# HGRN2 on one NeuronCore: a level's products and elementwise steps for both halves of the tokens at once

## The chip, the cores and the metric

The kernel is one program on one NeuronCore of a Trainium2 chip. A core has five engines that run their own instruction streams and wait for each other through semaphores: TensorE (PE in the rows; its weight loads are listed as PEld), VectorE (DVE), ScalarE (ACT), GpSimd (POOL) and SyncE (SP, which issues most transfers). The metric is the device time of one execution in microseconds (us); lower is better.

## The reference, cut to what matters

Four layers of a decoder trunk run over 1024 tokens of width 1024, each with a normalisation before it and a gated residual add behind it. Layers 0 and 3 use HGRN2, layer 1 windowed attention, layer 2 gated DeltaNet. The change touches HGRN2 alone (8 heads of 128 channels, chunks of tokens):

```python
def hgrn2_scan(q, k, v, log_f):
    ...
    def step(S, inp):
        q_, k_, v_, lf = inp
        b = jnp.cumsum(lf, axis=-2)
        diff = b[..., :, None, :] - b[..., None, :, :]
        dec = jnp.exp(jnp.where(causal[:, :, None], diff, -jnp.inf))
        A = jnp.einsum('bhtd,bhsd,bhtsd->bhts', q_, k_, dec)
        o = jnp.einsum('bhts,bhse->bhte', A, v_) + jnp.einsum('bhtd,bhde->bhte', q_ * jnp.exp(b), S)
        b_last = b[..., -1:, :]
        S = jnp.exp(b_last)[..., 0, :, None] * S + jnp.einsum('bhsd,bhse->bhde', k_ * jnp.exp(b_last - b), v_)
        return S, o
```

The matrix A weighs token t against an earlier token s with a product of decays that differs from channel to channel, so it is no plain matmul.

## The kernel before, in words

The 1024 tokens are two halves of 512 (`HT`), a half is four chunks of 128 (`NC`). Arrays lie with channels on the 128 partitions and tokens along the free axis.

`hgrn2` works head by head. For each head two generators are woven together by `weave`, which takes the next piece from the stream that is least far along: `mix(h)`, the recurrence of head h, and `proj` and `proj_v`, the input projections of the next head (and of the z gate), with a few pieces of the next layer's modulation (`side`) between them. The projections are long rows of fp32r matmuls (`proj_ps` of 512 columns, `projt_ps` of 256), three for each product because weights and activations are split into a high and a low part (L196 to L198). What is written here only sets priorities: Tile, the layer that schedules the program, orders each engine's instructions when the program is built. Level products stand in `burst()`, a priority raised by 4000, so that they go as soon as they are ready; `mix` as a whole is raised by 150 (`PRH`).

`mix` does this for one half at a time (`for hf in halves`), in this order:

- **levels.** A is built inside each 128-token chunk by products over blocks of 2, 8, 32 and 128 tokens. Level 0 multiplies q against kg (16 small matmuls of 48 columns into `lev_ps`, L1004); VectorE takes the diagonal (L1010) and the neighbour (L1012, a predicated copy under `lmask`) into `hg_A`. Then, for l = 1, 3, 5: ScalarE and VectorE form `hg_X` from `hg_qf` and the decays `hg_F` (L1031 to L1033), TensorE multiplies X against kg (16 matmuls, L1004; for l = 5 twelve of 96, 64 or 32 columns, L1050), VectorE takes three pieces into A (L1039), and VectorE brings F, qf and kg up by two levels (L1056 to L1061). The products of a level read kg as the level before left it, and kg may be changed only when they are done.
- **at.** At l = 5 GpSimd copies A into the diagonal blocks of `hg_at` (four copies, L1044) and ScalarE copies the products into the others (three copies, L1053).
- **scan.** Transposes of kg (L1067), then chunk by chunk the output (`o_ps`: S times qf, L1077, and v times at, L1078) and the state (`s_ps`, L1082, and `hg_S`, L1087), then the norm, a transpose back (L1099) and the gate (L1102).

So a head runs levels of half 0, scan of half 0, levels of half 1, scan of half 1. `hg_q`, `hg_f`, `hg_kg` and `hg_qf` are tiles of one half, in three buffers each. The last head (h = 7) calls `mix` for each half by itself, beside the output projection.

Of the kernel before, what the change touches and what calls it, by code (L numbers as in the profile page):

```python
# [84 lines left out]
class Trunk:  # L85
# [175 lines left out]
    def level_masks(self):  # L261


        nc, const = self.nc, self.const
        si, ti, a, b = (self.np.tile([P, P], I32, name=f"lm{n}") for n in range(4))
        nc.gpsimd.iota(si, pattern=[[0, P]], base=0, channel_multiplier=1)
        nc.gpsimd.iota(ti, pattern=[[0, NC], [1, 32]], base=0, channel_multiplier=0)
        nc.vector.tensor_scalar(si, si, 31, None, ALU.bitwise_and)
        lmask = const.tile([P, 7 * 64], U8, name="lmask")
        self.eye32 = const.tile([P, P], F32, name="eye32")  # L270
        nc.vector.tensor_tensor(a, ti, si, ALU.subtract)
        nc.vector.tensor_scalar(self.eye32, a, 0, None, ALU.is_equal)
# [651 lines left out]
    def hgrn2(self, i, side):  # L924
# [4 lines left out]
        mp = st.enter_context(self.tc.tile_pool(name=f"hg{i}", bufs=1, reuse_waits="tile"))  # L929
        nc = self.nc  # L930
        H, HA, NG = 8, 7, 4 * NC
        bufs = {"X": 1, "q": 3, "f": 3, "kg": 3, "qf": 3, "tmp": 3, "v": 3, "zs": 3, "kht": 1, "ohi": 1, "olo": 1}

        def tl(tag, dt=F32):
            return mp.tile([P, HT], dt, name=f"hg_{tag}", tag=tag, bufs=bufs[tag])

        def proj(h, d, parts, halves=(0, 1)):

            def ev_q(hf, ps):
                sg = tl("tmp")  # L940
                nc.scalar.activation(sg, ps, AF.Sigmoid)
                d["q", hf] = mp.tile([P, NG, 48], F32, name="hg_q", tag="q", bufs=bufs["q"])
                gr = lambda x: x.rearrange("p (g t) -> p g t", g=NG)
                nc.vector.tensor_tensor(d["q", hf][:, :, :32], gr(ps), gr(sg), ALU.mult)

            def ev_f(hf, ps):
                f, kg, qf = tl("f"), tl("kg"), tl("qf")
# [7 lines left out]
                q = d["q", hf]  # L955
# [5 lines left out]
                d["f", hf], d["kg", hf], d["qf", hf] = f, kg, qf  # L961
# [28 lines left out]
        def mix(h, d, halves=(0, 1)):  # L990
            S = d.get("S")
            for hf in halves:
                q, f, kg, qf, v = (d[x, hf] for x in ("q", "f", "kg", "qf", "v"))
                at = ats[hf]
                A = mp.tile([P, P], F32, name="hg_A", tag="hg_A", bufs=2)

                def products(x, kg):

                    pl = self.psum("lev", "lev_ps", 2)[:, :192]
                    with self.burst():  # L1000
                        for c in range(NC):
                            for g in range(4):
                                gs = slice(g * 32, (g + 1) * 32)
                                nc.tensor.matmul(pl[gs, c * 48:(c + 1) * 48], kg[:, c * P + g * 32:c * P + (g + 1) * 32], x[:, 4 * c + g, :], start=True, stop=True)  # L1004
                    return pl


                pl = products(q, kg)
                pv = pl.rearrange("p (c t) -> p c t", c=NC)
                nc.vector.tensor_tensor(A.rearrange("p (c t) -> p c t", c=NC), pv[:, :, :32], self.eye32.rearrange("p (c t) -> p c t", c=NC), ALU.mult)  # L1010
                av = A.rearrange("p (c n b) -> p c n b", c=NC, b=2)[:, :, :, 1]
                nc.vector.copy_predicated(av, self.lmask[0, 1].rearrange("p (c n) b j -> p c (n b j)", c=NC), pv[:, :, 32:])  # L1012
                yield 700
                fv, kv = (x.rearrange("p (n b) -> p n b", b=2) for x in (f, kg))
                F = mp.tile([P, HT // 2], F32, name="hg_F", tag="hg_F", bufs=2)
                nc.vector.tensor_tensor(F, fv[:, :, 0], fv[:, :, 1], ALU.mult)
                nc.vector.tensor_tensor(kv[:, :, 0], kv[:, :, 0], fv[:, :, 1], ALU.mult)
# [3 lines left out]
                for l in (1, 3, 5):  # L1021
                    j = 1 << l
                    nq = HT // (4 * j)
                    qv, kv = (x.rearrange("p (n b j) -> p n b j", b=4, j=j) for x in (qf, kg))
                    Fv = F.rearrange("p (n b) -> p n b", b=4)
                    bc = lambda b0, b1, w: Fv[:, :, b0:b1, None].to_broadcast([P, nq, w, j])

                    nx = 7 if j == 32 else 6
                    X = mp.tile([P, NC * 7 * 32], F32, name="hg_X", tag="hg_X", bufs=bufs["X"])[:, :nq * nx * j]
                    xv = X.rearrange("p (n b j) -> p n b j", b=nx, j=j)  # L1030
                    nc.scalar.copy(xv[:, :, 0:3, :], qv[:, :, 1:4, :])  # L1031
                    nc.vector.tensor_tensor(xv[:, :, 3:5, :], qv[:, :, 2:4, :], bc(1, 3, 2), ALU.mult)
                    nc.vector.tensor_tensor(xv[:, :, nx - 1, :], xv[:, :, 4, :], bc(1, 2, 1)[:, :, 0, :], ALU.mult)  # L1033
                    if j < 32:
                        pl = products(X.rearrange("p (g t) -> p g t", g=NG), kg)
                        pv = pl.rearrange("p (n b j) -> p n b j", b=6, j=j)
                        av = A.rearrange("p (n b j) -> p n b j", b=4, j=j)
                        for n, b0 in ((1, 0), (2, 3), (3, 5)):
                            nc.vector.copy_predicated(av[:, :, n:, :], self.lmask[l, n], pv[:, :, b0:b0 + 4 - n, :])  # L1039
                        yield 700  # L1040
                    else:
                        for g in range(4):
                            gs = slice(g * 32, (g + 1) * 32)
                            nc.gpsimd.tensor_copy(at[gs, :, gs], A[gs].rearrange("p (c t) -> p c t", c=NC))  # L1044
                        pl = self.psum("lev", "lev_ps", 2).rearrange("p (c b t) -> p c b t", c=NC, t=32)
                        with self.burst():
                          for c in range(NC):
                            for g in range(3):
                                gs = slice(g * 32, (g + 1) * 32)
                                nc.tensor.matmul(pl[gs, c, g + 1:, :], kg[:, c * P + g * 32:c * P + (g + 1) * 32], xv[:, c, g::3 if g == 0 else 4 - g, :][:, :3 - g, :] if g < 2 else xv[:, c, 2:3, :], start=True, stop=True)  # L1050
                        for g in range(3):
                            gs = slice(g * 32, (g + 1) * 32)
                            nc.scalar.copy(at[gs, :, (g + 1) * 32:], pl[gs, :, g + 1:, :].rearrange("p c b t -> p c (b t)"))  # L1053
                        yield 900
                    for b in (2, 1):
                        nc.vector.tensor_tensor(Fv[:, :, b], Fv[:, :, b], Fv[:, :, b + 1], ALU.mult)  # L1056
                    nc.vector.tensor_tensor(qv[:, :, 1, :], qv[:, :, 1, :], bc(0, 1, 1)[:, :, 0, :], ALU.mult)
                    nc.vector.tensor_tensor(qv[:, :, 2:4, :], xv[:, :, 3::nx - 4, :], bc(0, 1, 2), ALU.mult)
                    nc.vector.tensor_tensor(kv[:, :, 0:3, :], kv[:, :, 0:3, :], bc(1, 4, 3), ALU.mult)
                    Fn = mp.tile([P, nq], F32, name="hg_F", tag=f"hg_F{l}", bufs=2)  # L1060
                    nc.vector.tensor_tensor(Fn, Fv[:, :, 0], Fv[:, :, 1], ALU.mult)  # L1061
                    F = Fn
                    yield 1
# [60 lines left out]
        drain(side)  # L1124
        for hf in range(2):
# [322 lines left out]
```

## Time and profile before

| | |
|---|---|
| median of 3 runs | 2753.58 us (2751.43 to 2759.05) |
| profiled execution: its time, its span | 2752.67 us, 2751.0 us |
| PE busy | 2669.9 us, 97% |
| PEld busy | 2147.2 us, 78% |
| DVE busy | 2001.3 us, 73% |
| ACT busy | 1224.1 us, 44% |
| POOL busy | 133.8 us, 5% |
| mean granted TensorE clock | 0.993 |

The span runs from the first to the last instruction, so the execution's time is a little longer. Busy times are unions of instruction spans; a matmul's span is longer than its spacing to the next, since matmuls overlap, so a busy PE need not be at its peak. Layer 0's heads run from about 64 to 530 us of the span, layer 3's from about 2185 to 2640 us, and each layer's last head and output projection follow.

### The profile page before, as it was taken

The numbers are of one execution on the slowest core, as the hardware profiler recorded it, in microseconds if no ns is written. First come the engines' busy times: TensorE is split into PE (matmuls) and PEld (weight loads), VectorE is DVE, ScalarE is ACT, GpSimd is POOL, SyncE is SP. The second block draws the span as 40 slices with busy tenths as digits, with TensorE's granted clock in tenths as the row PEclk, the third lists the DMA queues.
The fourth block names the chain that finished last, engine by engine and source line by source line (L and its number), as shares of the span: only waits on it lengthen the run. The fifth ranks groups of instructions, "written<-read, shape, count | busy, mean of one in ns | idle before, by whom it ended". The sixth has DMA issues, their size and how long they took to land.

```text
span 2751.0 us, 51716 instructions
## 1 busy us (share of the span) xinstructions
PE 2669.9 (97%) x19217; PEld 2147.2 (78%) x19217; DVE 2001.3 (73%) x5669; ACT 1224.1 (44%) x3107; POOL 133.8 (5%) x352
## 2 busy tenths in 40 slices
PE   8999999998999999899999999999999999999999
PEld 4878888778878767677788877787778888887877
DVE  6685765778677778677898798988875757556575
ACT  4332333444445565444546455555543433333342
POOL 0000100000000000001101001100000000000000
PEclk9999999999999999999999999999999999999999
DMA  6232222344223243324343343432463211111133
GB/s 237 82 103 82 66 85 74 118 129 146 62 85 97 77 149 91 116 74 111 94 127 101 92 123 101 116 104 77 150 188 119 81 54 40 51 46 49 46 120 112
DMA packets 347666, 273.30 MB, mean 99 GB/s; under 512 B 68963, under 2 KB 276246, under 8 KB 347414
## 3 DMA queue, kind: packets, MB, share of 16 engines
q1 hardware_dynamic: 347126, 268.95, 32.8%
q8 instruction: 151, 2.47, 0.4%
q14 instruction: 101, 0.83, 0.1%
q0 software_dynamic: 288, 1.05, 0.1%
HBM read 224.77 MB, written 45.15 MB: 98 GB/s over the span
## 4 chain that ended last, share of the span: by engine, by line
PE 76%; DVE 11%; DMA 6%; ACT 4%; issue 2%; SPq 1%; POOL 0%; DVEq 0%; ACTq 0%
PE proj_ps L196 10%; PE proj_ps L198 10%; PE proj_ps L197 10%; PE outp_ps L198 4%; PE outp_ps L196 4%; PE outp_ps L197 4%; PE projt_ps L197 3%; PE projt_ps L198 3%; PE projt_ps L196 3%; DMA ada_w<-in_ada_w_dram 2%; PE lev_ps L1004 2%; DVE gd_tb L617 1%; PE pv_ps L1330 1%; DVE w_lo L172 1%; PE w_ps L859 1%
## 5 line engine op out<-in xcount | busy, mean ns | idle before, releaser
L196 PE MATMUL proj_ps<-hhi,w_hi 128*128 128x512 f32 x1664 | 686.1, 412 | 11.2 <-ACT gd_tb L615 8.6
L197 PE MATMUL proj_ps<-hlo,w_hi 128*128 128x512 f32 x1664 | 675.5, 406 | 0.0
L198 PE MATMUL proj_ps<-hhi,w_lo 128*128 128x512 f32 x1664 | 674.0, 405 | 0.0
L196 PEld LDWEIGHTS proj_ps<-hhi,w_hi 128*128 128x128 f32 x1664 | 315.5, 190 | 68.3 <-ACT gd_tb L615 11.0
L198 PEld LDWEIGHTS proj_ps<-hhi,w_lo 128*128 128x128 f32 x1664 | 314.9, 189 | 59.1 <-issue 1.2
L197 PEld LDWEIGHTS proj_ps<-hlo,w_hi 128*128 128x128 f32 x1664 | 315.3, 190 | 53.0 <-issue 1.4
L172 DVE TENSOR_TENSOR w_lo<-w_raw,w_hi 128x512 fp32r<-128x512 f32 x332 | 223.1, 675 | 168.2 <-ACT w_hi L171 165.6
L171 ACT CAST w_hi<-w_raw 128x512 fp32r<-128x512 f32 x332 | 201.9, 611 | 307.8 <-PE proj_ps L197 183.1
L197 PE MATMUL projt_ps<-w_lo,hhi 128*128 128x256 f32 x896 | 256.1, 290 | 5.8 <-DVE w_lo L172 5.8
L196 PE MATMUL projt_ps<-w_hi,hhi 128*128 128x256 f32 x896 | 256.1, 291 | 0.5 <-ACT w_hi L171 0.5
L198 PE MATMUL projt_ps<-w_hi,hlo 128*128 128x256 f32 x896 | 255.4, 290 | 0.0
L196 PE MATMUL outp_ps<-o_hi,w_hi 128*128 128x512 f32 x576 | 229.3, 400 | 2.9 <-ACT o_hi L1156 1.9
L198 PE MATMUL outp_ps<-o_hi,w_lo 128*128 128x512 f32 x576 | 228.0, 398 | 1.4 <-DVE w_lo L175 1.4
L197 PE MATMUL outp_ps<-o_lo,w_hi 128*128 128x512 f32 x576 | 228.8, 398 | 0.2
L197 PEld LDWEIGHTS projt_ps<-w_lo,hhi 128*128 128x128 f32 x896 | 170.7, 192 | 9.2 <-DVE w_lo L172 6.8
L196 PEld LDWEIGHTS projt_ps<-w_hi,hhi 128*128 128x128 f32 x896 | 170.5, 192 | 3.8 <-issue 1.2
L198 PEld LDWEIGHTS projt_ps<-w_hi,hlo 128*128 128x128 f32 x896 | 170.6, 192 | 2.3 <-issue 1.4
L617 DVE SCALAR_TENSOR_TENSOR gd_tb<-gd_xs,taps,gd_tb 128x512 f32<-128x512 f32 x192 | 144.2, 751 | 25.1 <-ACT gd_tb L615 21.5
L174 ACT ACTIVATE w_hi<-w_raw,par 128x512 fp32r<-128x512 f32 (+1 forms) x136 | 94.7, 698 | 142.9 <-PE outp_ps L197 98.8
L196 PEld LDWEIGHTS outp_ps<-o_hi,w_hi 128*128 128x128 f32 x576 | 108.6, 189 | 27.0 <-ACT o_hi L1156 3.9
L175 DVE SCALAR_TENSOR_TENSOR w_lo<-w_raw,par,w_hi 128x512 fp32r<-128x512 f32 (+1 forms) x136 | 96.8, 716 | 42.8 <-ACT w_hi L174 41.5
L198 PEld LDWEIGHTS outp_ps<-o_hi,w_lo 128*128 128x128 f32 x576 | 108.6, 189 | 24.2 <-DVE w_lo L175 1.9
(388 smaller groups left out, 4918.5 us busy)
## 6 DMA issues: line engine op xcount, KB each, us to landing
ada_w<-in_ada_w_dram SPq DMA_DIRECT2D x160, 256.0 KB, 2.8
w_raw<-in_hg_in_w_dram SPq DMA_DIRECT2D x136, 256.0 KB, 2.8
w_raw<-in_gd_in_w_dram SPq DMA_DIRECT2D x108, 256.0 KB, 3.1
o_in<-od SPq DMA_DIRECT2D x72, 256.0 KB, 3.3
w_raw<-in_gd_out_w_dram SPq DMA_DIRECT2D x64, 256.0 KB, 2.8
w_raw<-in_sw_in_w_dram SPq DMA_DIRECT2D x48, 256.0 KB, 3.0
w_raw<-in_hg_out_w_dram SPq DMA_DIRECT2D x40, 256.0 KB, 2.9
ada_w<-in_ada_w_dram SPq DMA_DIRECT2D x8, 1024.0 KB, 10.0
```

The source lines that it names most:

```text
L171: nc.scalar.copy(hi, raw)
L172: nc.vector.tensor_tensor(lo, raw, hi.bitcast(F32), ALU.subtract)
L174: nc.scalar.activation(hi, raw, AF.Copy, scale=scale)
L175: nc.vector.scalar_tensor_tensor(lo, raw, scale, hi.bitcast(F32), ALU.mult, ALU.subtract)
L196: mm(out, a[0], b[0], start=start, stop=False)
L197: mm(out, a[0], b[1], start=False, stop=False)
L198: mm(out, a[1], b[0], start=False, stop=stop)
L617: nc.vector.scalar_tensor_tensor(y, xs[:, j:j + HT], w(j), y, ALU.mult, ALU.add)
L859: nc.tensor.matmul(po[:, hd[a]], dd["u"][a, hf][:, cs], rhs, start=True, stop=True)
L1004: nc.tensor.matmul(pl[gs, c * 48:(c + 1) * 48], kg[:, c * P + g * 32:c * P + (g + 1) * 32], x[:, 4 * c + g, :], start=True, stop=True)
L1330: nc.tensor.matmul(po[a * 64:(a + 1) * 64], vg[:, n + 1 - nkb + b, :], p4[:, :, a, :], start=b == 0, stop=b == nkb - 1)
```

## The change

A new generator `levels(d, halves)` does the levels and the at copies for all given halves before any scan; `mix` calls it first and keeps only the scan in its loop over halves. For heads 0 to 6 both halves are given, so A, X and F are twice as wide, 32 products of 48 columns go into one `lev_ps` tile, and each elementwise instruction covers 1024 tokens in place of 512. At l = 5 there is one `lev_ps` tile for each half, and the GpSimd and ScalarE copies stay apart by half. q, f, kg and qf become tiles of 1024 tokens, one buffer for even and one for odd heads (the even heads' in a pool of their own, `mp0`, closed after head 6). The masks get the double width, the unit mask `eye32` is 32 columns read again and again. The last head still gives one half at a time.

```diff
-        bufs = {"X": 1, "q": 3, "f": 3, "kg": 3, "qf": 3, "tmp": 3, "v": 3, "zs": 3, "kht": 1, "ohi": 1, "olo": 1}
+        bufs = {"X": 1, "tmp": 3, "v": 3, "zs": 3, "kht": 1, "ohi": 1, "olo": 1}
...
-                f, kg, qf = tl("f"), tl("kg"), tl("qf")
+                if hf == 0:
+                    d.update((x, (mp if h % 2 else mp0).tile([P, T], F32, name="hg_" + x, tag=x, bufs=1)) for x in ("f", "kg", "qf"))
+                f, kg, qf = (d[x][:, hf * HT:(hf + 1) * HT] for x in ("f", "kg", "qf"))
...
+        def levels(d, halves):
+
+            C, c0 = NC * len(halves), NC * halves[0]
+            W = C * P
...
+            def products(x):
+
+                pl = self.psum("lev", "lev_ps", 2)[:, :C * 48]
+                with self.burst():
+                    for c in range(C):
+                        for g in range(4):
+                            gs = slice(g * 32, (g + 1) * 32)
+                            nc.tensor.matmul(pl[gs, c * 48:(c + 1) * 48], kg[:, c * P + g * 32:c * P + (g + 1) * 32], x[:, 4 * c + g, :], start=True, stop=True)
+                return pl
...
+            yield 700 * len(halves)
...
+            for l in (1, 3, 5):
+                j = 1 << l
+                nq = W // (4 * j)
...
+                nc.scalar.copy(xv[:, :, 0:3, :], qv[:, :, 1:4, :])
+                nc.vector.tensor_tensor(xv[:, :, 3:5, :], qv[:, :, 2:4, :], bc(1, 3, 2), ALU.mult)
...
+                else:
+                    pls = [self.psum("lev", "lev_ps", 2).rearrange("p (c b t) -> p c b t", c=NC, t=32) for hf in halves]
+                    with self.burst():
+                        for c in range(C):
+                            for g in range(3):
+                                gs = slice(g * 32, (g + 1) * 32)
+                                x = (xv[:, c, 0:7:3, :], xv[:, c, 1:5:3, :], xv[:, c, 2:3, :])[g]
+                                nc.tensor.matmul(pls[c // NC][gs, c % NC, g + 1:, :], kg[:, c * P + g * 32:c * P + (g + 1) * 32], x, start=True, stop=True)
+                    for hf, pl in zip(halves, pls):
...
+                        for g in range(4):
+                            gs = slice(g * 32, (g + 1) * 32)
+                            nc.gpsimd.tensor_copy(ats[hf][gs, :, gs], Ah[gs])
+                        for g in range(3):
+                            gs = slice(g * 32, (g + 1) * 32)
+                            nc.scalar.copy(ats[hf][gs, :, (g + 1) * 32:], pl[gs, :, g + 1:, :].rearrange("p c b t -> p c (b t)"))
+                    yield 900 * len(halves)
...
         def mix(h, d, halves=(0, 1)):
             S = d.get("S")
+            yield from levels(d, halves)
             for hf in halves:
-                q, f, kg, qf, v = (d[x, hf] for x in ("q", "f", "kg", "qf", "v"))
...
+                at, v, F = ats[hf], d["v", hf], d["F", hf]
+                kg, qf = (d[x][:, hf * HT:(hf + 1) * HT] for x in ("kg", "qf"))
```

The built programs show what the scheduler makes of it. TensorE has the same 15345 matmuls. A run of level products, uninterrupted by other matmuls, is called a burst here; there are 121 bursts before and 85 after. VectorE has 5195 instructions in place of 5671, ScalarE 2547 in place of 2589. In layers 1 and 2 the order is the same on every engine.

On TensorE, in head 1 of layer 0, the products of level 3 stand among projection matmuls before (one half):

```order
L197 MATMUL proj_ps<-hlo,w_hi 128x512
L198 MATMUL proj_ps<-hhi,w_lo 128x512
L1004 MATMUL lev_ps<-hg_X,hg_kg 32x48 x16
L196 MATMUL proj_ps<-hhi,w_hi 128x512
L197 MATMUL proj_ps<-hlo,w_hi 128x512
```

and after (both halves):

```order
L197 MATMUL proj_ps<-hlo,w_hi 128x512
L198 MATMUL proj_ps<-hhi,w_lo 128x512
L1012 MATMUL lev_ps<-hg_X,hg_kg 32x48 x32
L196 MATMUL proj_ps<-hhi,w_hi 128x512
L197 MATMUL proj_ps<-hlo,w_hi 128x512
```

Two bursts of 16 have become one of 32. Between this burst and the one of level 1 ahead of it stand 11 projection matmuls before and 13 after.

On VectorE, in the same head, this is what stands between the last X step of level 1 and that of level 3 before (one half):

```order
L1056 TENSOR_TENSOR hg_F<-hg_F 128x64
L1058 TENSOR_TENSOR hg_qf<-hg_X,hg_F 128x64x4
L1056 TENSOR_TENSOR hg_F<-hg_F 128x64
L172 TENSOR_TENSOR w_lo<-w_raw,w_hi 128x512
L1039 COPY_PREDICATED hg_A<-lmask,lev_ps 128x16x6
L1059 TENSOR_TENSOR hg_kg<-hg_kg,hg_F 128x64x6
L1039 COPY_PREDICATED hg_A<-lmask,lev_ps 128x16x4
L1061 TENSOR_TENSOR hg_F<-hg_F 128x64
L1039 COPY_PREDICATED hg_A<-lmask,lev_ps 128x16x2
L1032 TENSOR_TENSOR hg_X<-hg_qf,hg_F 128x16x16
L1057 TENSOR_TENSOR hg_qf<-hg_qf,hg_F 128x16x8
L1033 TENSOR_TENSOR hg_X<-hg_X,hg_F 128x16x8
```

and after (both halves):

```order
L1068 TENSOR_TENSOR hg_F<-hg_F 128x128
L1069 TENSOR_TENSOR hg_qf<-hg_qf,hg_F 128x128x2
L1068 TENSOR_TENSOR hg_F<-hg_F 128x128
L1070 TENSOR_TENSOR hg_qf<-hg_X,hg_F 128x128x4
L1073 TENSOR_TENSOR hg_F<-hg_F 128x128
L1048 COPY_PREDICATED hg_A<-lmask,lev_ps 128x32x6
L1040 TENSOR_TENSOR hg_X<-hg_qf,hg_F 128x32x16
L1048 COPY_PREDICATED hg_A<-lmask,lev_ps 128x32x4
L1041 TENSOR_TENSOR hg_X<-hg_X,hg_F 128x32x8
L1048 COPY_PREDICATED hg_A<-lmask,lev_ps 128x32x2
L1071 TENSOR_TENSOR hg_kg<-hg_kg,hg_F 128x128x6
```

The eleven steps are the same, each with twice the elements; the weight split (L172) that stood among them has gone elsewhere.

On TensorE, behind the last level of head 1's first half, before (the last of the twelve products, then level 0 of the other half):

```order
L1050 MATMUL lev_ps<-hg_X,hg_kg 32x32
L1004 MATMUL lev_ps<-hg_q,hg_kg 32x48 x16
L196 MATMUL proj_ps<-hhi,w_hi 128x512
L197 MATMUL proj_ps<-hlo,w_hi 128x512
L1078 MATMUL o_ps<-hg_v,hg_at_592 128x128
L198 MATMUL proj_ps<-hhi,w_lo 128x512
```

and after, behind the 24 products of both halves:

```order
L1057 MATMUL lev_ps<-hg_X,hg_kg 32x32
L198 MATMUL proj_ps<-hhi,w_lo 128x512
L1098 MATMUL o_ps<-hg_v,hg_at_595 128x128
L196 MATMUL proj_ps<-hhi,w_hi 128x512
L197 MATMUL proj_ps<-hlo,w_hi 128x512
L198 MATMUL proj_ps<-hhi,w_lo 128x512
L196 MATMUL proj_ps<-hhi,w_hi 128x512
L1087 MATMUL kh_ps<-ident,hg_kg 128x128 x4
```

The first output product, which reads the at copies of half 0, has moved from two projection matmuls behind its burst to one. It stands so in 8 of the 14 heads with merged levels; before, an output product followed a burst of 12 and 16 as closely in 6 places that the change does away with.

## Rows read from the trace of the kernel before

**Rows 1.** The page: engines (busy us, share, instructions) and the chain that ended last.

```profile
PE 2669.9 (97%) x19217; PEld 2147.2 (78%) x19217; DVE 2001.3 (73%) x5669; ACT 1224.1 (44%) x3107; POOL 133.8 (5%) x352
...
PE 76%; DVE 11%; DMA 6%; ACT 4%; issue 2%; SPq 1%; POOL 0%; DVEq 0%; ACTq 0%
```

**Rows 2.** Busy time of the engines by stage; the last columns are clock and transfers.

```profile
64.00:530.00 466.00, 460.40 (x4312) 381.90 (x4310) 316.50 (x1014) 159.87 (x378) 31.37 (x65) 1.00 0.28 84
...
2185.00:2640.00 455.00, 451.35 (x4243) 372.58 (x4241) 290.57 (x970) 158.76 (x377) 26.45 (x64) 1.00 0.16 48
```

**Rows 3.** What PE waited for in layer 0: total us, times, longest.

```profile
PE ot_ps L1099 <- DVE hg_tmp L1095: 2.6, 8, 0.8
...
PE o_ps L1078 <- ACT hg_at L1053: 0.6, 2, 0.3
```

**Rows 4.** PE in order of time in layer 0: start, us, line, records.

```profile
151.15 0.55 PE L1004 MATMUL lev_ps<-hg_X,hg_kg 128*32 128x48 f32 x32
...
154.03 0.39 PE L198 MATMUL proj_ps<-hhi,w_lo 128*128 128x512 f32 x1
154.34 0.55 PE L1004 MATMUL lev_ps<-hg_X,hg_kg 128*32 128x48 f32 x32
154.82 0.50 PE L196 MATMUL proj_ps<-hhi,w_hi 128*128 128x512 f32 x1
155.16 0.40 PE L197 MATMUL proj_ps<-hlo,w_hi 128*128 128x512 f32 x1
...
156.77 0.39 PE L198 MATMUL proj_ps<-hhi,w_lo 128*128 128x512 f32 x1
157.09 0.77 PE L1050 MATMUL lev_ps<-hg_X,hg_kg 128*32 128x96 f32 x23
...
157.69 0.25 PE L1050 MATMUL lev_ps<-hg_X,hg_kg 128*32 128x96 f32 x1
157.69 0.58 PE L1004 MATMUL lev_ps<-hg_q,hg_kg 128*32 128x48 f32 x27
158.20 0.50 PE L196 MATMUL proj_ps<-hhi,w_hi 128*128 128x512 f32 x1
158.54 0.40 PE L197 MATMUL proj_ps<-hlo,w_hi 128*128 128x512 f32 x1
```

**Rows 5.** PE in order of time, around a burst of the last level.

```profile
405.24 0.39 PE L197 MATMUL proj_ps<-hlo,w_hi 128*128 128x512 f32 x1
405.47 0.39 PE L198 MATMUL proj_ps<-hhi,w_lo 128*128 128x512 f32 x1
405.78 0.85 PE L1050 MATMUL lev_ps<-hg_X,hg_kg 128*32 128x96 f32 x24
406.56 0.50 PE L196 MATMUL proj_ps<-hhi,w_hi 128*128 128x512 f32 x1
406.90 0.39 PE L197 MATMUL proj_ps<-hlo,w_hi 128*128 128x512 f32 x1
```

**Rows 6.** DVE in order of time, between the two bursts of group 4.

```profile
150.71 0.28 DVE L1033 TENSOR_TENSOR hg_X<-hg_X,hg_F 128x128 f32<-128x128 f32 x1
...
151.61 0.69 DVE L172 TENSOR_TENSOR w_lo<-w_raw,w_hi 128x512 fp32r<-128x512 f32 x1
152.21 0.30 DVE L1039 COPY_PREDICATED hg_A<-lmask,lev_ps 128x96 f32<-128x96 uint8 x1
...
153.28 0.42 DVE L1032 TENSOR_TENSOR hg_X<-hg_qf,hg_F 128x256 f32<-128x256 f32 x1
153.62 0.28 DVE L1057 TENSOR_TENSOR hg_qf<-hg_qf,hg_F 128x128 f32<-128x128 f32 x1
153.82 0.28 DVE L1033 TENSOR_TENSOR hg_X<-hg_X,hg_F 128x128 f32<-128x128 f32 x1
```

**Rows 7.** ACT in order of time, behind the burst of group 5.

```profile
406.70 1.11 ACT L1053 COPY hg_at<-lev_ps 32x384 f32<-32x384 f32 x3 [1.79 <-PE lev_ps L1050]
```

**Rows 8.** PE in order of time, behind the bursts of group 4.

```profile
159.26 0.46 PE L1078 MATMUL o_ps<-hg_v,hg_at 128*128 128x128 f32 x2 [0.32 <-ACT hg_at L1053]
```

More of the change, by code (lines that the diff above doesn't have):

```diff
@@ L264, in level_masks @@
         nc, const = self.nc, self.const
-        si, ti, a, b = (self.np.tile([P, P], I32, name=f"lm{n}") for n in range(4))
-        nc.gpsimd.iota(si, pattern=[[0, P]], base=0, channel_multiplier=1)
-        nc.gpsimd.iota(ti, pattern=[[0, NC], [1, 32]], base=0, channel_multiplier=0)
+        W = 2 * NC * 32
+        si, ti, a, b = (self.np.tile([P, W], I32, name=f"lm{n}") for n in range(4))
+        nc.gpsimd.iota(si, pattern=[[0, W]], base=0, channel_multiplier=1)
+        nc.gpsimd.iota(ti, pattern=[[0, 2 * NC], [1, 32]], base=0, channel_multiplier=0)
         nc.vector.tensor_scalar(si, si, 31, None, ALU.bitwise_and)
-        lmask = const.tile([P, 7 * 64], U8, name="lmask")
-        self.eye32 = const.tile([P, P], F32, name="eye32")
+        lmask = const.tile([P, 7 * W // 2], U8, name="lmask")
+        self.eye32 = const.tile([P, 32], F32, name="eye32")
         nc.vector.tensor_tensor(a, ti, si, ALU.subtract)
-        nc.vector.tensor_scalar(self.eye32, a, 0, None, ALU.is_equal)
+        nc.vector.tensor_scalar(self.eye32, a[:, :32], 0, None, ALU.is_equal)
         self.lmask, o = {}, 0
@@ L988, in proj_v @@
                     ds[h]["v", hf] = v[:, :, (h % 2) * P:(h % 2 + 1) * P]
+        def levels(d, halves):
+            C, c0 = NC * len(halves), NC * halves[0]
+            W = C * P
+            ws, gs_ = slice(c0 * P, c0 * P + W), slice(4 * c0, 4 * (c0 + C))
+            q = d["q"][:, gs_, :]
+            f, kg, qf = (d[x][:, ws] for x in ("f", "kg", "qf"))
+            A = mp.tile([P, 2 * P], F32, name="hg_A", tag="hg_A", bufs=2)[:, :C * 32]
+            def products(x):
[6 more added lines that the diff above has]
+                return pl
+            pl = products(q)
+            pv = pl.rearrange("p (c t) -> p c t", c=C)
+            nc.vector.tensor_tensor(A.rearrange("p (c t) -> p c t", c=C), pv[:, :, :32], self.eye32[:, None, :].to_broadcast([P, C, 32]), ALU.mult)
+            av = A.rearrange("p (c n b) -> p c n b", c=C, b=2)[:, :, :, 1]
+            nc.vector.copy_predicated(av, self.lmask[0, 1][:, :C * 16].rearrange("p (c n) -> p c n", c=C), pv[:, :, 32:])
+            yield 700 * len(halves)
+            fv, kv = (x.rearrange("p (n b) -> p n b", b=2) for x in (f, kg))
+            F = mp.tile([P, HT], F32, name="hg_F", tag="hg_F", bufs=1)[:, :W // 2]
+            nc.vector.tensor_tensor(F, fv[:, :, 0], fv[:, :, 1], ALU.mult)
+            nc.vector.tensor_tensor(kv[:, :, 0], kv[:, :, 0], fv[:, :, 1], ALU.mult)
+            for l in (1, 3, 5):
+                j = 1 << l
+                nq = W // (4 * j)
+                qv, kv = (x.rearrange("p (n b j) -> p n b j", b=4, j=j) for x in (qf, kg))
+                Fv = F.rearrange("p (n b) -> p n b", b=4)
+                bc = lambda b0, b1, w: Fv[:, :, b0:b1, None].to_broadcast([P, nq, w, j])
+                nx = 7 if j == 32 else 6
+                X = mp.tile([P, 2 * NC * 7 * 32], F32, name="hg_X", tag="hg_X", bufs=bufs["X"])[:, :nq * nx * j]
+                xv = X.rearrange("p (n b j) -> p n b j", b=nx, j=j)
+                nc.scalar.copy(xv[:, :, 0:3, :], qv[:, :, 1:4, :])
+                nc.vector.tensor_tensor(xv[:, :, 3:5, :], qv[:, :, 2:4, :], bc(1, 3, 2), ALU.mult)
+                nc.vector.tensor_tensor(xv[:, :, nx - 1, :], xv[:, :, 4, :], bc(1, 2, 1)[:, :, 0, :], ALU.mult)
+                if j < 32:
+                    pl = products(X.rearrange("p (g t) -> p g t", t=48))
+                    pv = pl.rearrange("p (n b j) -> p n b j", b=6, j=j)
+                    av = A.rearrange("p (n b j) -> p n b j", b=4, j=j)
+                    for n, b0 in ((1, 0), (2, 3), (3, 5)):
+                        m = self.lmask[l, n][:, :C * (32 // (4 * j)) * (4 - n) * j].rearrange("p (n b j) -> p n b j", b=4 - n, j=j)
+                        nc.vector.copy_predicated(av[:, :, n:, :], m, pv[:, :, b0:b0 + 4 - n, :])
+                    yield 700 * len(halves)
+                else:
[7 more added lines that the diff above has]
+                    for hf, pl in zip(halves, pls):
+                        Ah = A.rearrange("p (c t) -> p c t", c=C)[:, (hf - halves[0]) * NC:(hf - halves[0] + 1) * NC, :]
+                        for g in range(4):
[5 more added lines that the diff above has]
+                    yield 900 * len(halves)
+                for b in (2, 1):
+                    nc.vector.tensor_tensor(Fv[:, :, b], Fv[:, :, b], Fv[:, :, b + 1], ALU.mult)
+                nc.vector.tensor_tensor(qv[:, :, 1, :], qv[:, :, 1, :], bc(0, 1, 1)[:, :, 0, :], ALU.mult)
+                nc.vector.tensor_tensor(qv[:, :, 2:4, :], xv[:, :, 3::nx - 4, :], bc(0, 1, 2), ALU.mult)
+                nc.vector.tensor_tensor(kv[:, :, 0:3, :], kv[:, :, 0:3, :], bc(1, 4, 3), ALU.mult)
+                Fn = mp.tile([P, 2 * HT // (4 * j)], F32, name="hg_F", tag=f"hg_F{l}", bufs=2 if l == 5 else 1)[:, :nq]
+                nc.vector.tensor_tensor(Fn, Fv[:, :, 0], Fv[:, :, 1], ALU.mult)
+                F = Fn
+                yield 1
+            d.update((("F", hf), F[:, n * NC:(n + 1) * NC]) for n, hf in enumerate(halves))
@@ L990, in mix @@
         def mix(h, d, halves=(0, 1)):
             S = d.get("S")
+            yield from levels(d, halves)
             for hf in halves:
-                q, f, kg, qf, v = (d[x, hf] for x in ("q", "f", "kg", "qf", "v"))
[L994 to L1005, printed above, removed]
@@ L1008, in mix @@
[L1008 to L1014, printed above, removed]
@@ L1015, in mix @@
[L1015 to L1063, printed above, removed]
```

15 lines of the change are left out of this document (9 added, 6 removed).

## The prediction, made before the changed kernel was run

> **What bounds the kernel now.** I read the page first: PE is busy for 97% of the span, DVE for 73%, and the chain that ended last is 76% PE and 11% DVE [rows 1]. These are averages over four layers, so the busy times by stage come next. The changed heads run in two stretches. In layer 0's, 466 us long, PE is idle for 466 - 460.4 = 5.6 us, in layer 3's for 455 - 451.35 = 3.65 us, while DVE works for 316.5 and 290.6 us, some two thirds [rows 2]. The granted clock is 1.00 in both, the upper level of 2.4 GHz; nothing here is priced by it. So DVE time as such is worth at most those 9.25 us; what counts is time on PE. A busy PE is not a PE at its peak, so I went to PE's timeline to see how matmuls start after each other. Projection matmuls of 512 columns start every 0.23 us (405.24 to 405.47, [rows 5]). A burst of level products breaks that beat, and the beat tells its price.
>
> **The change part by part.**
>
> *Fewer bursts (a gain on PE).* From the last projection before a lone burst of 16 to the second behind it: 154.03 to 155.16 = 1.13 us [rows 4]; two beats of 0.228 would be 0.456, so the burst costs 0.67. A lone burst of twelve products of the last level: 405.47 to 406.90 = 1.43, less 0.456 = 0.97 [rows 5]. Where the two stand together (157.09, twelve, and from about 157.6 sixteen), 156.77 to 158.54 = 1.77, less 0.456 = 1.31 [rows 4]. Apart they would cost 0.67 + 0.97 = 1.64, so joining two bursts gives back 0.33 us: a part of a burst's price is paid at its edges (the last product to the first projection, and a first projection that takes 0.34 to the next in place of 0.23), not by product. The orders have 36 fewer bursts: 36 x 0.33 = -12.0 us. The bounds: nothing, if edges cost as much inside a wider burst; -14, if also the other matmul runs that vanish between projections are counted (42 runs at 0.33).
>
> *Fewer DVE and ACT instructions (off the path, mostly).* 34 DVE instructions a head go, in 14 heads: 476, which is what the orders have. What one costs beyond its elements is read from starts: 512 elements hold DVE for 0.60 (151.61 to 152.21), 256 for 0.34, 128 for 0.20 [rows 6], so 0.08 is fixed and the rest is about 1 ns an element. 476 x 0.08 = 38 us of DVE, 6% of the 607 us above. PE runs beside it, and hides it; what PE waits for is little: 2.6 us for the norm's result before a transpose in layer 0, 0.6 for the at copies [rows 3]. I take -1.0 us, with 0 and all of PE's idle time, -9.25, as bounds. ACT's 42 copies less go the same way; I give them nothing of their own.
>
> The Trainium skill, "VectorE: DVE Perf Modes", section on the TRN2 errata, says that each VectorE instruction has a fixed cost, measured there as about 150 cycles at 0.96 GHz, exposed between instructions, so that few large tiles are cheaper. By it 476 x 0.157 = 75 us of DVE would go, an estimate from that page. The rows agree with its duration (0.42 for 256 elements) but not with the exposure: the next instruction starts 0.08 before the end. The sum stays with the rows; with the page's figure it would move only if DVE set the end (the third rival).
>
> *Longer DVE chains between bursts (a loss).* A burst waits for the X and kg of its level, and PE's queue is in order: all projections behind it wait too. Before, DVE needs from the end of L1033 at 150.99 to its end at 154.10 = 3.11 us [rows 6], of which 0.60 is a weight split; so 2.51 for the eleven steps that the order shows. PE goes from burst to burst in 154.34 - 151.15 = 3.19 [rows 4], and comes 0.24 after DVE: no wait. After, the eleven steps have twice the elements and no split among them: 2 x 2.51 - 11 x 0.08 = 4.14. PE's time grows by two projections and the wider burst: 3.19 + 0.46 + 0.34 = 3.99. The shortest lag from DVE to a burst's start here is 151.15 - 150.99 = 0.16, so the next burst can start 4.14 us after the last, 0.15 late. The other two gaps of a head vary: in every second head the orders leave 5 us of projections ahead of level 1. I charge one gap a head: 14 x 0.15 = +2.1 us. Bounds: 0, and all 42 merged bursts late by 0.15, +6.3.
>
> *The first output product comes sooner behind the at copies (a loss).* It reads what ACT copies out of half 0's last products, 1.11 us of work [rows 7]; GpSimd's copies are ready earlier, since the row names ACT as what PE waited for [rows 8]. Before, such a product started at 159.26, 1.57 behind the last of those products at 157.69 [rows 4, 8], and PE stood idle for 0.32 of it. After, half 0's last product starts again 0.60 into the burst (157.09 to 157.69), so the output product can start at 2.17. PE would be there earlier: the lone burst takes 0.78 to its first projection [rows 5], twelve more products 0.64 (0.78 less the edge of 0.14), and 0.34 to the next: 1.76. It waits 0.41 in each of 8 heads: +3.3 us. The 6 places of before go: there the product was due 0.23 behind 158.54 and came 0.49 late at the worst, 0.6 us idle in two of them by the waits; between 0.6 and 2.9 in all, I take 1.7. Net +1.6, bounds 0 and +2.7.
>
> *The rest at nothing.* Wider masks are made on DVE and POOL at the start, while PE waits for transfers. The double-width tiles only loosen reuse between heads, at a price in space, not time. Head 7 is unchanged.
>
> The sum: -12.0 - 1.0 + 2.1 + 1.6 = -9.3. On the profiled execution's 2752.67 us (its span is 2751.0) that gives 2743.4; the median of the runs is 0.91 above that execution, so **2744 us**. About 0.3%, 8.3 us, is what a measurement of this kernel can tell from no change, so this forecast lies just beyond it.
>
> **The rivals.**
>
> *No change that can be told (chance 0.21).* The two losses are at their upper bounds, or an edge costs less than 0.33 when 64 records of one kind follow each other: -12.0 + 6.3 + 2.7 = -3.0, 2751 us. For it: after, DVE's need and PE's time between bursts are nearly equal (4.14 and 3.99). Against: they were before as well (3.11 and 3.19), and PE's idle time stayed at 1% [rows 2].
>
> A rule of the Trainium skill leads to the same side: "Perfetto Trace Analysis", section on the most-contended engine, says that matmul busy time does not tell how near TensorE is to its limit, and weight-load busy time does. PEld is busy for 381.9 of 466 us, 82% [rows 2]: room is left, so PE would be held by others and shorter bursts gain nothing: 2754 us. The steady beat of 0.23 with 1% of idle time speaks against it in these stretches; of the 0.21 it has 0.03.
>
> *Slower (0.07).* The scheduler placed the bursts too early for the doubled chains, and PE stands at each of the 42 merged bursts. The point from which this decides: a wait of (9.3 + 2.1) / 42 = 0.27 us at each eats the gain, 0.47 makes it slower by 8.3. At 0.6, which a second weight split of 0.60 in each chain would bring, 42 x 0.6 - 11.4 = +13.8: 2767. Against: the order above shows the split moved out.
>
> *More gain (0.14).* The shorter DVE queue takes away most of PE's idle time in the heads: -12.0 - 9.25 + about 2 = -19, 2734 us. For it: the largest wait is for DVE [rows 3]. Against: these waits are chains of short dependent steps (the norm), not a full queue.
>
> **How the numbers follow.** The forecast, -5 to -13 us (2740.5 to 2748.5), has 0.58. Of it some three fifths lie beyond 8.3 us: 0.36, with 0.14 from the last rival 0.50 faster; the rest, 0.22, with the first rival's 0.21 gives 0.43 for no change; 0.07 slower. The range for 8 in 10 goes from the last rival to the first: 2735 to 2753.
>
> **What would show it.** Right: 85 bursts, a merged one of 32 at about 1.01 us by the same beats, not 1.34; PE's starts around an output product at L1098 behind the last level late by some 0.4 with ACT's at copy (L1065) as its releaser; DVE's busy time lower by 30 to 75 us without PE's idle time in the heads changing much; layers 1 and 2 as long as before. Wrong: waits of PE at `lev_ps` that add up to over 5 us, a merged burst that costs twice a single one, or a new wait for weights (`w_lo`, `w_hi`).

## The result and the profile after

The changed kernel takes 2761.06 us (median of 22 runs, 2749.14 to 2771.25) against 2752.55 us of the kernel before on the same chips: ratio 1.0025, 95% interval 1.0015 to 1.0035. Measured again with 12 more runs: 1.0020 (1.0004 to 1.0036). That is 0.25% slower: little, but the interval lies clear of no change, and the time lies outside the range of 2735 to 2753; the forecast was 2744.

Page and two stages after, which answer to [rows 1, 2]. A stage's row has its length, then busy us and instructions of PE, PEld, DVE, ACT and POOL, then the granted clock, the busy share of the transfers and their GB/s:

```profile
PE 2664.9 (97%) x19217; PEld 2148.4 (78%) x19217; DVE 1965.6 (71%) x5193; ACT 1215.8 (44%) x3065; POOL 147.8 (5%) x352
PE 74%; DVE 14%; DMA 4%; ACT 4%; issue 2%; POOL 1%; SPq 0%; DVEq 0%; ACTq 0%; POOLq 0%
```

```profile
64.00:530.00 466.00, 451.81 (x4224) 377.71 (x4223) 290.56 (x747) 151.16 (x348) 35.76 (x60) 0.99 0.27 82
2185.00:2640.00 455.00, 449.94 (x4185) 374.94 (x4184) 269.81 (x722) 155.30 (x353) 32.75 (x60) 1.00 0.16 48
```

VectorE works 35.7 us less, as intended. PE is idle for 2759.5 - 2664.9 = 94.6 us, before 81.1; in layer 0's stretch 14.2 in place of 5.6. A second profile of the changed kernel (`after_again`) has 91.1 and 11.3. The merged burst costs what was forecast. PE after, around a burst of 32 products (two records for each):

```profile
159.33 0.39 PE L197 MATMUL proj_ps<-hlo,w_hi 128*128 128x512 f32 x1
159.65 0.89 PE L1012 MATMUL lev_ps<-hg_X,hg_kg 128*32 128x48 f32 x64
160.47 0.50 PE L198 MATMUL proj_ps<-hhi,w_lo 128*128 128x512 f32 x1
160.80 0.40 PE L196 MATMUL proj_ps<-hhi,w_hi 128*128 128x512 f32 x1
```

160.80 - 159.33 = 1.47, less two beats 1.01: 0.33 less than two bursts of 0.67. What came in its place are waits. What PE waited for after, in the whole span (total, times, longest):

```profile
PE o_ps L1098 <- POOL hg_at L1062: 5.5, 7, 2.3
...
PE o_ps L1097 <- DVE hg_S L1107: 3.3, 3, 1.3
PE ot_ps L1119 <- DVE hg_tmp L1115: 2.9, 7, 1.5
...
PE lev_ps L1057 <- DVE hg_kg L1071: 2.5, 1, 2.5
...
PE projt_ps L196 <- ACT hg_v L990: 1.8, 2, 1.1
...
PE lev_ps L1012 <- DVE hg_F L1068: 1.5, 5, 0.3
...
PE o_ps L1098 <- ACT hg_at L1065: 0.6, 2, 0.3
```

All but the norm's (`ot_ps`) and ScalarE's (`hg_at` L1065) are new. The one for `hg_kg` lies in layer 3's last head, which is not merged. One of the two longest waits for `hg_at`, on PE, GpSimd and VectorE:

```profile
285.83 1.48 PE L1057 MATMUL lev_ps<-hg_X,hg_kg 128*32 128x96 f32 x48
287.24 0.51 PE L198 MATMUL proj_ps<-hhi,w_lo 128*128 128x512 f32 x1
289.68 0.49 PE L1098 MATMUL o_ps<-hg_v,hg_at 128*128 128x128 f32 x2 [1.94 <-POOL hg_at L1062]
...
291.50 0.63 PE L198 MATMUL proj_ps<-hhi,w_lo 128*128 128x512 f32 x1
291.92 0.63 PE L196 MATMUL proj_ps<-hhi,w_hi 128*128 128x512 f32 x1
```

```profile
284.98 6.04 POOL L1062 COPY hg_at<-hg_A 32x128 f32<-32x128 f32 x8 [64.75 <-DVE hg_A L1048]
```

```profile
284.71 0.98 DVE L1071 TENSOR_TENSOR hg_kg<-hg_kg,hg_F 128x768 f32<-128x768 f32 x1
285.57 0.20 DVE L1068 TENSOR_TENSOR hg_F<-hg_F 128x8 f32<-128x8 f32 x1
285.66 0.45 DVE L1069 TENSOR_TENSOR hg_qf<-hg_qf,hg_F 128x256 f32<-128x256 f32 x1
286.00 0.20 DVE L1068 TENSOR_TENSOR hg_F<-hg_F 128x8 f32<-128x8 f32 x1
286.08 0.71 DVE L1070 TENSOR_TENSOR hg_qf<-hg_X,hg_F 128x512 f32<-128x512 f32 x1
286.68 0.19 DVE L1073 TENSOR_TENSOR hg_F<-hg_F 128x8 f32<-128x8 f32 x1
286.77 0.70 DVE L172 TENSOR_TENSOR w_lo<-w_raw,w_hi 128x512 fp32r<-128x512 f32 x1
287.38 1.05 DVE L1071 TENSOR_TENSOR hg_kg<-hg_kg,hg_F 128x768 f32<-128x768 f32 x1
```

GpSimd begins its eight copies at 284.98 and needs 6.04 us; PE reaches the first output product 2 us before half 0's four are done. This head and the one at 407 are the extremes: there half 0's four copies take 4.7 and 5.0 us. In ten of the 14 merged heads they take 2.6 us, and PE waits for them 0.3 us at most. A head of this kind, and the copies at the place of [rows 8] before:

```profile
215.65 4.58 POOL L1062 COPY hg_at<-hg_A 32x128 f32<-32x128 f32 x8 [42.50 <-DVE hg_A L1048]
```

```profile
156.51 1.85 POOL L1044 COPY hg_at<-hg_A 32x128 f32<-32x128 f32 x4 [34.64 <-DVE hg_A L1039]
```

Behind the long wait projections start every 0.42 us (291.50 to 291.92) in place of 0.23. The stages show why (columns as above; the third is the start of head 7):

```profile
290.80:294.20 3.40, 3.40 (x10) 2.62 (x9) 0.00 (x0) 0.00 (x0) 0.22 (x1) 0.50 0.11 38
413.70:417.00 3.30, 3.30 (x10) 2.52 (x9) 0.00 (x0) 0.00 (x0) 0.01 (x1) 0.50 0.18 60
536.60:543.30 6.70, 6.43 (x38) 5.26 (x39) 4.92 (x14) 2.85 (x6) 0.00 (x0) 0.50 0.48 156
```

The granted clock is 0.50, the lower level of 1.2 GHz, behind the waits of 1.94 and 2.29 us and at the start of head 7. A stretch of 3.4 us costs about 1.7. In head 7 PE waits three times within some 2 us (0.3, 0.7 and 0.4), but so it does in the kernel before (0.3, 0.7 and 0.2), and there the clock stays at 1.00; that this fall is the change's is not shown. Over the whole profiles the stretches at 0.50 add up to 38.6 us before and 48.5 after; half of the difference, 5.0 us, is what they can cost.

The clock falls in some executions and not in others, so times spread. In the runs of either kernel, 0.001 of mean granted clock goes with 2.4 us (a straight line through time and clock of each run). 34 runs of the changed kernel have mean 2760.3 us at clock 0.9903, 105 of the kernel before 2754.4 at 0.9924: 0.0021 x 2400 = 5.0 of the 5.9 us between them go with the clock. These means, not single profiles, are compared below; their standard error is 0.5 us for the kernel before, 0.9 for the changed one, 1 to 2 for the others. Between its three sets of runs the mean of the kernel before goes from 2753.0 to 2756.1, so a difference of some 3 us between two sets is not much.

### The profile page after: what moved, and what is told of

It reads as the page before. It is cut to its first block, busy times and chain, and to the rows that moved or that the text cites. A ratio compares the mean times of both kernels' runs of the same rounds, so it can differ in the third digit from the quotient of the medians.

```text
span 2759.5 us, 51174 instructions
## 1 busy us (share of the span) xinstructions
PE 2664.9 (97%) x19217; PEld 2148.4 (78%) x19217; DVE 1965.6 (71%) x5193; ACT 1215.8 (44%) x3065; POOL 147.8 (5%) x352
## 4 chain that ended last, share of the span: by engine, by line
PE 74%; DVE 14%; DMA 4%; ACT 4%; issue 2%; POOL 1%; SPq 0%; DVEq 0%; ACTq 0%; POOLq 0%
PE proj_ps L196 10%; PE proj_ps L197 10%; PE proj_ps L198 10%; PE outp_ps L198 4%; PE outp_ps L197 4%; PE outp_ps L196 4%; PE projt_ps L197 3%; PE projt_ps L198 3%; PE projt_ps L196 3%; DMA ada_w<-in_ada_w_dram 2%; DVE gd_tb L618 1%; DVE w_lo L172 1%; PE pv_ps L1351 1%; PE w_ps L860 1%; PE pt_ps L1345 1%
## 5 line engine op out<-in xcount | busy, mean ns | idle before, releaser
L172 DVE TENSOR_TENSOR w_lo<-w_raw,w_hi 128x512 fp32r<-128x512 f32 x332 | 223.6, 676 | 171.4 <-ACT w_hi L171 158.0
```

The source lines that it names most:

```text
L172: nc.vector.tensor_tensor(lo, raw, hi.bitcast(F32), ALU.subtract)
```

## The experiments

**GpSimd's copies made by ScalarE** (`diag_act`).

```diff
-nc.gpsimd.tensor_copy(ats[hf][gs, :, gs], Ah[gs])
+nc.scalar.copy(ats[hf][gs, :, gs], Ah[gs])
```

> The changed kernel, but the eight diagonal copies of a head are made by ACT in place of POOL; on PE only a few first output products stand one projection later. Theory A (POOL's small copies are held up while VectorE works through its double-width products of two SBUF tiles; one took 2.70 us where it takes 0.35 to 0.5 elsewhere): the two PE waits of 1.94 and 2.29 us in layer 0 shrink to 0.5 or less each, the two stretches behind them in which projections start every 0.43 us in place of 0.23 go too (1.4 us each), so 3.5 + 2.8 + some of the smaller waits = 6 to 8 us less than the changed kernel: 2753 to 2755. Theory B (the output product is simply placed too early, whoever copies; ACT then has 14 copies in a row): a wait of 1 us or more stays there, named ACT, and the time stays within 3 us of the changed kernel's 2761.

Median 2755.22, ratio to before 1.0010 (0.9995 to 1.0026); mean 2755.6 at clock 0.9921. The eight copies take 2.45 us on ScalarE. Yet the wait stays, now for ScalarE, since the other copies come behind them. Waits for the tile `hg_at`:

```profile
  PE o_ps L1098: 7.2, 8
```

After the change it was 6.1 us in 9 (3.9 in the second profile). So the time was forecast by A and the wait by B: PE waits as long in sum, but 1.2 us at the longest in place of 2.3, and in layer 0's heads the clock stays at 1.00. The gain of 4.7 us (standard error 2) is about that of the clock, 0.0018 x 2400 = 4.3. GpSimd alone is not the cause; `o_later` below asks whether it is where the product stands.

**Merged in layer 3 only** (`layer3_only`).

```diff
-            yield from levels(d, halves)
+            if i:
+                yield from levels(d, halves)
             for hf in halves:
+                if not i:
+                    yield from levels(d, (hf,))
```

> Levels of both halves at once in layer 3 only; layer 0 does them half by half as before, with the tiles of the change. Theory A (the loss sits in layer 0: PE idle +10.5 and low-clock stretches +6.8 against 5.8 saved on bursts; layer 3 nets a gain of about 4 up to its last projection and gives 2 back behind it): 2 to 4 us below the kernel before, 2748.5 to 2750.5. Theory B (the loss comes from the wider work itself, wherever it is): half of the change's loss, about 4 us above the kernel before, 2757.

Median 2756.64, ratio 1.0010 (0.9997 to 1.0024). That is between 0.8 us below the kernel before and 6.6 above: Theory A's 2 to 4 below lie outside, B's 4 above inside. But the mean, 2756.6 at clock 0.9911, is 2.2 above the kernel before, and 0.0013 x 2400 = 3.1 go with the clock; that the wider work itself costs time is not shown by it.

**The order without the merging** (`order_only`).

```diff
-            yield from levels(d, halves)
+            for hf in halves:
+                yield from levels(d, (hf,))
             for hf in halves:
```

> Both halves' levels ahead of both scans as in the change, but level by level for one half at a time: 16 products a burst and single-width elementwise steps. It has the change's order of levels and scans without the merging. Theory A (merging saves 0.33 us a join, and the waits for POOL come from merging, since half 0's copies here end long before its scan; the scans back to back cost the state waits, 3.3 us in layer 0): 12 us of bursts come back, 4 us of POOL waits and 3 to 7 us of low clock go: 2760 to 2766. Theory B (the order of the scans is what costs, 15 us or more): 2768 or more. Theory C (the order costs nothing, all loss is from double width): within 2 us of the kernel before, 2752.

Median 2752.47, ratio 1.0005 (0.9988 to 1.0021), mean 2754.6. Theory C: both halves' levels ahead of the scans cost nothing that this interval, 3 us below to 6 above, would show. PE's waits for `hg_S` are 1.3 us here in the whole span, 3.7 with merging, 0.5 before.

**The tiles alone** (`tiles_only`, and again `tiles_again`).

```diff
-            yield from levels(d, halves)
             for hf in halves:
+                yield from levels(d, (hf,))
```

> The change's tiles (1024 tokens for q, f, kg, qf, one buffer a parity, masks and unit mask), but levels and scan half by half as before. If the tiles cost nothing: within 2 us of the kernel before, 2750.5 to 2754.5. Rival: one buffer for even and one for odd heads makes the next head's gates wait for the last reader of the same parity, and part of the 8.5 us is theirs: 2755 or more.

Median 2759.48, ratio 1.0021 (1.0007 to 1.0035), though its profiled execution was among the fastest (span 2751.1).

> The run with the tiles alone once more. Its profiled execution had the span of the kernel before (2751.1) while the median of its runs lay 7.6 us higher. If the tiles cost nothing and the median was a matter of how many low-clock stretches fell into those runs: 2751 to 2756, mean granted clock 0.992 or more. If the tiles do cost: 2757 to 2762 again.

Median 2756.73, ratio 1.0012 (0.9998 to 1.0026), between its two forecasts. The 24 runs have mean 2758.7 at clock 0.9919, 4.3 us above the kernel before, of which the clock explains 1.2. Both profiles show a new wait at the start of each HGRN2 layer, for `hg_v`: 0.7 us in layer 0 and 1.1 in layer 3, 1.8 together. Every kernel with these tiles has it, the changed one too (its row stands above), and no profile of the kernel before. What is left, 1.3 us, is about the standard error. `order_only` has the same wait and measured no loss, with a standard error of 1.8.

**The first output product later** (`o_later`). Its priority is taken back, so that it stands behind the transposes and the state products; GpSimd copies as in the change.

```diff
-                    nc.tensor.matmul(po[:, cs], at[:, c, :], v[:, c, :], start=S is None, stop=True)
+                    with self.tc.high_priority(offset=-150 if S is None else 0):
+                        nc.tensor.matmul(po[:, cs], at[:, c, :], v[:, c, :], start=S is None, stop=True)
```

> The changed kernel, but the first output product of a head's half 0 loses its priority, so that it stands behind the transposes and the state products instead of one projection behind the last level; GpSimd still copies. Theory A (the placement exposes the copies, and PE's waits of 2 us there also cost granted clock): no wait for GpSimd's copies is left, 5.5 us of layer 0's and 1.2 us of layer 3's idle time go, the low-clock stretches at 291 and 414 us too; the 11 us saved on bursts show: 10 to 14 us below the changed kernel, 2747 to 2751. Theory B (something else, the waits for the state chain and for the norm, takes over as what is late): less than 4 us below the changed kernel, 2757 or more.

Median 2749.94, ratio 0.9986 (0.9970 to 1.0001). GpSimd is as slow as ever, and no output product waits for it. GpSimd, and who waited for the tile `hg_at` on PE's side:

```profile
285.53 5.84 POOL L1062 COPY hg_at<-hg_A 32x128 f32<-32x128 f32 x8 [67.15 <-DVE hg_A L1048]
```

```profile
  PEld lev_ps L1012: 1.1, 3
```

```profile
64.00:530.00 466.00, 458.16 (x4319) 384.63 (x4318) 298.82 (x778) 158.40 (x361) 36.82 (x64) 1.00 0.28 85
```

PE's idle time in layer 0 is 7.8 us in place of 14.2 (11.3 in the second profile). Theory A.

> The changed kernel with the later first output product once more, for a tighter comparison with the kernel before. If the 11 us saved on bursts are real and the placement was what ate them: 3 to 7 us below the kernel before again, 2747 to 2751. If the first result was a matter of few low-clock stretches: within 2 us of the kernel before.

Median 2751.40, ratio 0.9987 (0.9969 to 1.0006). Mean of both sets (23 runs, without one whose clock record does not fit its time): 2750.4 at 0.9918, 9.9 below the changed kernel and 4.0 below the kernel before. Either set's interval still reaches no change from the kernel before; the 4.0 of both have a standard error of 1.3. Against the changed kernel, PE's idle time over the span falls from 94.6 and 91.1 us in its two profiles to 87.1 and 88.2, by 5.2 in the mean, and 0.0015 x 2400 = 3.6 go with the clock: 8.8 of the 9.9. The waits for `hg_at` are gone (6.1 and 3.9), those for `hg_S` fall from 3.7 to 1.5, and those for `hg_q` rise from 0.9 to 2.3.

**The same edit in the kernel before** (`before_later`).

> The kernel before, unmerged, with the same later first output product. Theory A (merging gives the gain, the later product only stops the loss that merging brings; before, these products waited 0.75 us in all): within 2 us of the kernel before. Theory B (the later product is a gain by itself, merging gives nothing): 3 us or more below the kernel before.

Median 2756.04 against 2756.00, ratio 0.9993 (0.9975 to 1.0011). By the median it is Theory A: the later product gives nothing without the merging. The interval, 7 us below to 3 above, does not by itself exclude B's 3 us.

**GpSimd's copies twice** (`diag_twice`).

```diff
                             nc.gpsimd.tensor_copy(ats[hf][gs, :, gs], Ah[gs])
+                            nc.gpsimd.tensor_copy(ats[hf][gs, :, gs], Ah[gs])
```

> The changed kernel with every diagonal copy of GpSimd made twice; the orders are the same otherwise, the first output products stay one projection behind the last level. Theory A: half 0's four copies more take 1.2 to 3 us, so PE waits for GpSimd at all eight such products, 12 to 20 us more idle time in sum, and the granted clock falls behind several of them: 15 to 30 us above the changed kernel, 2775 to 2790, mean granted clock 0.988 or less. Theory B (the copies are not what PE waits for): under 5 us more.

Median 2787.64, ratio 1.0107 (1.0082 to 1.0132), mean 2786.8 at clock 0.9868. Who waited for `hg_at`, and three of seven stretches at the lower clock, each right behind such a wait (an eighth wait, of 2.19 us at 2268.73, has none):

```profile
  PE o_ps L1099: 25.2, 10
```

```profile
127.30:130.60 3.30, 3.30 (x12) 2.61 (x11) 0.00 (x0) 1.10 (x2) 1.31 (x5) 0.50 0.23 83
178.50:181.80 3.30, 3.30 (x12) 2.62 (x11) 0.56 (x1) 1.10 (x2) 1.44 (x5) 0.50 0.08 32
424.30:427.60 3.30, 3.30 (x9) 2.62 (x8) 0.00 (x0) 0.00 (x0) 1.77 (x7) 0.50 0.00 2
```

25.2 - 6.1 = 19.1 us of waits (21.3 by the second profile) and 0.0035 x 2400 = 8.4 of clock make 27.5 (29.7); measured is 26.5. Theory A.

**GpSimd beside VectorE, by itself** (`probe`).

> The changed kernel with a test behind its end: GpSimd makes four times eight copies of 32x128 f32, once with VectorE idle, then while VectorE runs 24 instructions of 128x512 f32: products of two SBUF tiles, then products of one SBUF tile and a constant, then products of a PSUM and an SBUF tile. Its whole time is longer by the test. Theory A (an instruction with two SBUF inputs holds GpSimd off): eight copies alone 3 to 4 us; beside two-input instructions the copies take several times as long, 1 us or more each, or end only with VectorE's row; beside PSUM inputs as alone. Theory B (GpSimd's copies were slow for another reason): four times the same.

2804.63 us with the test. Only a part of it ran as planned: three sets of copies had VectorE idle or nearly so, the fourth ran beside 20 products of two SBUF tiles, none beside the other kinds.

```profile
2755.14 3.49 POOL L1458 COPY pr_d<-pr_g 32x128 f32<-32x128 f32 x8 [0.39 <-DVE pr_g L1456]
2759.02 5.78 POOL L1458 COPY pr_d<-pr_g 32x128 f32<-32x128 f32 x8 [0.39 <-DVE pr_g L1456]
```

By single records a copy takes 0.28 to 0.29 us alone and 0.66 to 0.69 beside the products, one copy to each product. For this kind the direction is Theory A's, but 2.3 times as long is less than the 1 us or more that it gave.

**Both kernels once more** (`after_again`, `before_again`).

> The changed kernel once more, for a second profile of it. If the places with PE waits of 1.9 us or more decide where the granted clock falls, the stretches at about 291 and 414 us (behind the first output products of heads 2 and 4) are there again or have moved to others of such places; the waits themselves are the same within 0.2 us; time 2758 to 2764.

Median 2760.00, ratio 1.0020 (1.0004 to 1.0036). This profile has the wait at 288.69 again, 1.75 us, without a fall of the clock behind it; the one near 412 is 0.28 us here. So such a wait makes the fall possible, not certain. The forecast failed: one of the two waits did not return, and no stretch. The wait that did, and the stretch behind it:

```profile
288.69 0.38 PE L1098 MATMUL o_ps<-hg_v,hg_at 128*128 128x128 f32 x1 [1.75 <-POOL hg_at L1062]
```

```profile
288.70:292.10 3.40, 3.40 (x16) 2.88 (x17) 0.69 (x1) 0.09 (x1) 1.14 (x4) 1.00 0.36 119
```

> The kernel before against itself, for a second profile of it and for the size of a difference that means nothing: within 2.5 us of its own median; low-clock stretches in layer 0 only where PE waits 0.9 us or more.

Median 2755.74, ratio 0.9995 (0.9978 to 1.0011), as expected; layer 0 has no stretch at the lower clock.

## Why the prediction was wrong, point by point

*Fewer bursts, -12.0: right.* The beat above gives 0.33 a join. In the profile of `after_again`, whose heads hold no low-clock stretch, PE's time from the first to the last projection of layers 0 and 3, less its waits over 0.06 us, is 4.5 and 5.5 us shorter than before: 10.1 in all.

*VectorE's relief, -1.0: right as far as it went.* 35.7 us less busy against 38 worked out; the wait for the norm before a transpose is 2.9 and 1.7 us over the span in the two profiles of the changed kernel, 3.5 and 3.3 in those of the kernel before.

*Longer chains between bursts, +2.1: right in kind.* Waits for `hg_F` are 1.5 us in 5, up to 0.33 each where 0.15 was worked out, in some heads only. With two smaller waits the merged bursts wait 3.0 us, before 1.4. The sign of being wrong, over 5 us at `lev_ps`, is reached only with the 2.5 us in the last head of layer 3, which is not merged; `order_only` has that wait too.

*The first output product behind the at copies, +1.6: the step that failed.* It said "GpSimd's copies are ready earlier, since the row names ACT as what PE waited for" [rows 8]. That row is of a place with single-width VectorE work, where four copies ended in 1.9 us. Beside the double-width products half 0's four took 2.6 us in most merged heads, and 4.7 and 5.0 in two. ScalarE was near its estimate: at the wait shown above its three copies were done about 2.0 us into the burst (2.17 was worked out), GpSimd's four 3.8. So PE waited less than the 0.41 us charged in seven of nine places (0.2 to 0.3), and 1.94 and 2.29 us in the other two. Waits for `hg_at` went from 0.6 to 6.1 us (+5.5 in place of +1.6; +3.3 in the second profile, which has one long wait). Undoing the placement (`o_later`) took all of it back, doubling the copies quadrupled it.

*"Nothing here is priced by" the clock: failed too.* The 5.0 us that go with the clock are a third of the 15.2 that the sum is off (-9.3 forecast, +5.9 by the means). That the clock was 1.00 before, in stretches where the longest wait was 0.8 us [rows 2, 3], said nothing about waits of 2.

*The scans back to back: not in the sum.* Waits for `hg_S`, the state, rose from 0.5 to 3.7 us over the span; 3.3 of these are three waits in layer 0. In two of them the state's step stands in VectorE's order behind a step of the next layer's modulation (`ada_acc`), for which VectorE waits idle until a transfer lands; in the third, behind a weight split that waits for ScalarE. VectorE and PE at one of the two:

```profile
437.94 0.75 DVE L406 SCALAR_TENSOR_TENSOR ada_acc<-ada_w,par,ada_acc 128x512 f32<-128x512 f32 x1 [1.16 <-DMA ada_w<-in_ada_w_dram]
438.61 0.34 DVE L1107 SCALAR_TENSOR_TENSOR hg_S<-hg_S,hg_F,s_ps 128x128 f32<-128x128 f32 x1
```

```profile
439.09 0.35 PE L1097 MATMUL o_ps<-hg_S,hg_qf 128*128 128x128 f32 x1 [0.94 <-DVE hg_S L1107]
```

None stands behind a widened instruction. Why merging brings these meetings, and `order_only` fewer of them, is not shown.

*The rest at nothing: wrong for the tiles.* They were to cost "space, not time"; the wait for `hg_v` that comes with them is 1.8 us. The tiles alone measured 4.3 (standard error about 1), of which 1.2 go with the clock.

Together, in the profiled pair: -10.1 + 13.5 of idle time + 5.0 of clock = 8.4, measured 8.5. The rivals: "no change" came nearest in size, but not by its mechanism; "slower" had the sign, but the waits at merged bursts that it needed, over 11 us, are 3.0. The Trainium skill, "Perfetto Trace Analysis", section on identifying the most-contended engine, has weight-load busy time as a measure of how near TensorE is to its limit. What the prediction made of it, that shorter bursts give nothing, does not fit: PE's time on the same work fell by 10.1 us.

## What to carry to other kernels

Merging steps shortens the work and lengthens each instruction; look first at the small copies on other engines that used to slip in between, and at where their reader stands. Price a new wait on PE with the granted clock that may fall behind it, not with its own length alone. When a merged version is no faster, move the reader: here one priority turned 0.25% slower into about 0.14% faster, by the mean of two sets of runs.

## What the hardware showed that was not expected

A 32x128 copy on GpSimd takes 0.29 us alone, 0.67 beside VectorE's products of two SBUF tiles, and 2.64 while seven of these follow each other with every start ahead of the previous end (284.98 to 287.62); on ScalarE 0.30. But at 215.65, beside the same products in the same order, the first copy took 0.88 us, and in the second profile no copy of the head at 284 took over 2.19. What decides how soon a copy gets in between is not shown. The Trainium skill, "SBUF — State Buffer", section on the two separate sides, says that GpSimd and a VectorE instruction with two SBUF inputs take a shared port pair by an exclusive lock for a whole instruction. The copies of the test agree (0.67 is about the product's 0.69); its products showed no delay, 0.69 us beside the copies and behind them. In the kernel VectorE's short products were not all alike: those of 128x8 took 0.28 us at 216.27, where copies got in between, and 0.20 at 285.57, where none did.

The granted clock fell to 0.50 at single PE waits of 1.94 and 2.29 us, and at seven of the eight lengthened waits of `diag_twice` (2.19 to 4.33 us); at one of 2.19 us there, and at 1.75 us in `after_again`, it did not.
